# Layer 0's up projection in seven products for eight, and the w_down sums of both layers in DRAM

## The chip, the cores and the metric

The kernel runs on one core of a Trainium2 chip. The metric is the device time of one execution in microseconds (us); lower is better. The engines of the core are TensorE (PE, its weight loads PEld), VectorE (DVE), ScalarE (ACT), GpSimd (POOL) and SyncE (SP); each runs its own queue in order, and DMAs are issued from the queues of SP, ACT and POOL.

## What is computed

One inference step through two post-norm layers on 640 tokens (128 of a prompt, 512 of a sample), width 1024. Each layer modulates its input, mixes it (a state-space scan, a short convolution and an attention, which this change leaves alone), projects it with w_out, normalises, and runs an MLP of 4096 hidden columns with a squared ReLU. All data is float32.

```python
def trunk_layer(x, mod, p, lam_init, theta, prefix_k, prefix_v, s0_f, s0_b):
    sh1, sc1, g1, sh2, sc2, g2 = jnp.split(mod, 6, axis=-1)
    u = x * (1.0 + sc1) + sh1
    m, k, v, s_f, s_b = mixer(u, p, lam_init, theta, prefix_k, prefix_v, s0_f, s0_b)
    x = layer_norm(ALPHA * x + g1 * m, p['ln1_g'], p['ln1_b'])
    h = x * (1.0 + sc2) + sh2
    f = jnp.square(jax.nn.relu(h @ p['w_up'])) @ p['w_down']
    x = layer_norm(ALPHA * x + g2 * f, p['ln2_g'], p['ln2_b'])
    return x, k, v, s_f, s_b
```

The modulation vectors `mod` are a product of a conditioning vector with w_mod (1024 by 6144 per layer).

## The kernel before

Tokens stand in five tiles of 128. Every float32 product is made of three float32r products: each operand is split into a high part (ScalarE rounds it) and a low part (VectorE subtracts), and TensorE adds high x high, high x low and low x high in PSUM. `XH` and `XL` hold the two parts of the transposed activations, 8 blocks of 128 channels by 640 tokens.

Weights come from DRAM by SP into three `raw` tiles of 128 x 1024 and are split into units `hi`/`lo` (five of each in the pool `wp`), two blocks of 128 rows by 512 columns per unit.

The MLP goes through the hidden columns in groups. In layer 1 (`fast`) there are eight groups of 512; in layer 0 four groups of 1024. A group has an up projection, whose result is squared and split into `ah`/`al`, and a w_down run over five token tiles and two halves of 512 output columns.

- Layer 0: `up_block` and `ch_block`, dense, tokens in pieces of 384 and 256; the square's high part is cast on VectorE (line 1254, `V.tensor_copy`). `tok_block` runs w_down one half of columns after the other. `ev_dn` copies the first group's product into `acc[t]` in SBUF on ScalarE and adds the others on VectorE (line 1482).
- Layer 1: the first group is dense too, in two halves of 320 tokens; then `token_sums` and `token_sums_in_place` make sums and differences of the four quarters of the activations (halves of the tokens by halves of the channels), and each later group is two calls of `fast_pair`. A pair makes 256 hidden columns by seven products of 4 x 3 matmuls of 320 columns (with weight differences T1 to T4, built and split on VectorE and ScalarE) in place of eight. `dn_fast` does the w_down run: the first four items (token tile, half of columns) are half done for a start, then finished one by one; PSUM banks alternate between the pools `mm` and `tp`.

After the last group's up projection `acc` is multiplied by the gate row `grow` and added to ALPHA x `res` (two VectorE operations of 128 x 1024 per token tile); the last w_down run adds to `res` by `residual`, then comes the layer norm. The tiles `acc[0]` and `acc[1]` also hold the rows of the layer norm (`norm_rows`), the pool `gr` holds two gate rows, loaded by ScalarE's queue.

In layer 0 a generator, `mod_steps_sum`, works out the modulation of layer 1 (seven pieces of 1024 columns of w_mod) beside the MLP: SP loads 128 x 512 tiles `ws` into three buffers, VectorE multiplies and adds each into two accumulators `ma` (line 109), and per piece four matmuls `pmod`, a copy `mrow` and four transposes `pmt` end it. `spread(FU)` after each up eviction and `spread(FD)` after each w_down eviction move the generator on by that many steps; `fill_all` drains it. Its VectorE instructions carry a lower priority by LATE = 100 places.

The order on each engine's queue is fixed ahead of the run by a scheduler that goes by program order and these priorities. A tile with n buffers makes its next writer wait until the one n before has been used up.

Of the kernel before, what the change touches and what calls it, by code (L numbers as in the profile page):

```python
# [35 lines left out]
FZ, FU, FD = 2, .7, 3  # L36
# [5 lines left out]
LATE, EARLY = 100, 50  # L42
# [3 lines left out]
ORDER, N_HALF = (4, 3, 0, 1, 2), 4  # L46
# [12 lines left out]
def build(ctx: ExitStack, tc: tile.TileContext, I, O):  # L59
# [159 lines left out]
    def mod_steps_sum(pieces, pool):  # L219
# [4 lines left out]
        def small(name):  # L224
            return pool.tile([P, 4, P], F32, tag="u", name=name, bufs=3).rearrange("p a b -> p (a b)")
# [11 lines left out]
        for l, pc in pieces:  # L237
            acc = [pool.tile([P, 1024], F32, tag="xn", name=f"ma{l}_{pc}_{s}", bufs=2) for s in range(2)]
# [51 lines left out]
    def fill_all():  # L290
        while fillers:
            fill()
# [166 lines left out]
    xspill = dp.tile([TOK, D], F32, name="xspill")  # L459

# [154 lines left out]
    for l in range(DEPTH):  # L615
# [533 lines left out]

        def norm_rows(i):  # L1150
            out = []
            for j in range(2):
                r = acc[j]
# [62 lines left out]
        ubufs[0] = 5 if l + 1 == DEPTH else 3  # L1216
# [10 lines left out]
        if l + 1 < DEPTH:  # L1227
            next_end = ctx.enter_context(ExitStack())
            ep = next_end.enter_context(tc.tile_pool(name=f"kv{l + 1}", bufs=1, side=side_of(None), reuse_waits="tile"))
        op, op_end = open_pool("op")  # L1230
# [10 lines left out]
        extra = {} if fast else {"more": op, "early": EARLY}  # L1241
# [5 lines left out]
        def squared(r, hv, lv, src=None):  # L1247
# [3 lines left out]
            if fast:  # L1251
                act(hv, r)
            else:
                V.tensor_copy(hv, r)
# [5 lines left out]
        def up_block(g, b, ah, al):  # L1260
            blk = load_block(f"up{l}_{g}_{b}", w_up, 0, [(g * hg + b * 512, 512)], **extra)

            def ev_up(ct, half, ps):
                nm = f"relu{l}_{g}_{b}_{ct}_{half}"
                if fast:
                    o, m, r = half * H, H, room(nm)
                else:
                    o, m = (0, NA) if half == 0 else (NA, NB)
                    r = op.tile([P, NA], F32, tag="relu", name=nm, bufs=3)[:, :m]
# [3 lines left out]
            ch_block(f"up{l}_{g}_{b}", blk, ev_up, na=H if fast else NA)  # L1273
# [63 lines left out]
        def fast_pair(g, j, ah, al):  # L1337
# [32 lines left out]
            b = unit(1, op, 2, "c")  # L1370
# [13 lines left out]
            def out(r, ct, half, src=None):  # L1384
                o = H * half
                squared(r, ah[i + ct][:, o:o + H], al[i + ct][:, o:o + H], src)
# [25 lines left out]
        def dn_fast(g, stat, blks, evs):  # L1412

            items = [(t, c) for c in range(2) for t in ORDER]
            if g == ng - 1:
                items.sort(key=lambda x: ORDER.index(x[0]))
# [22 lines left out]

        ends = []  # L1440
        for g in range(ng):
            ah, al = a_tiles(g, hg // P)
            if fast and g:
                for j in range(2):
                    fast_pair(g, j, ah, al)
                if g == ng // 2:
                    gate_rows(1)
            else:
                for b in range(hg // 512):
                    up_block(g, b, ah, al)  # L1450
                    if g == 0 and b == 0:
                        with tc.high_priority(offset=-LATE if fast else 0):
                            for t, mv in later:
                                affine(rows, t, mv)
                        if fast:
                            with tc.high_priority(offset=-LATE):
                                token_sums()
                    if g == ng // 2 and b == 0:
                        gate_rows(1)
                if fast:  # L1460
                    token_sums_in_place()
            if g == ng - 1:
                for t in range(NT):
                    tt(acc[t], acc[t], grow[min(t, 1)], ALU.mult)
# [112 lines left out]
```

## Time and profile before

| | us |
|---|---|
| median of 3 runs | 1599.15 |
| lowest, highest run | 1598.96, 1604.01 |
| the profiled execution, its own time | 1600.18 |
| the profiled execution, its span | 1598.4 |
| TensorE busy in the span | 1558.9 |
| VectorE busy in the span | 1165.1 |
| ScalarE busy in the span | 768.6 |
| GpSimd busy in the span | 38.5 |

The profile is of one execution; the span runs from its first to its last instruction, and 1.8 us lie around it. Busy time is the time in which an engine executes an instruction. The granted clock of TensorE is full in almost all of the span. The MLP of layer 0 runs from about 392 to 841 us of the span, that of layer 1 from about 1167 us to the end.

### The profile page before, as it was taken

Reading aid. Unit: us, or ns where it says so; the run is one execution under the profiler, and the core shown is the slowest. Engines: PE = TensorE matmul, PEld = TensorE weight load, DVE = VectorE, ACT = ScalarE, POOL = GpSimd, SP = SyncE. Lnnn points to the kernel's source line nnn. Section 1 sums busy time; section 2 is a strip of 40 time slices with the busy share of each in tenths; the row PEclk is TensorE's granted clock in tenths of the full one; section 3 lists DMA queues with packets and bytes.
Section 4 is the critical chain, followed back from the end, with each engine's and each line's share of the span. In section 5 each row is a group of like instructions: output and inputs, shape, how many; then the busy total and the mean of one; then the engine's idle time right before and its main releaser. Section 6 shows DMA issues by size and latency. Waiting matters only on the chain.

```text
span 1598.4 us, 23756 instructions
## 1 busy us (share of the span) xinstructions
PE 1558.9 (98%) x9088; PEld 1373.1 (86%) x9088; DVE 1165.1 (73%) x2122; ACT 768.6 (48%) x1610; POOL 38.5 (2%) x68
## 2 busy tenths in 40 slices
PE   6999999999999999999999999999999999999997
PEld 3799957978989979979978999898798899988995
DVE  2589868778858478499376788898797566556687
ACT  3368735427422413314245587654486355434543
POOL 0000100000000000000000000000000000000001
PEclk9999999999999999999999999999999999999998
DMA  9641177342555355364226410524222233122311
GB/s 325 181 167 54 36 252 260 126 154 75 164 194 187 105 170 159 126 198 140 71 73 183 169 41 14 185 100 150 81 85 88 67 105 98 61 67 92 106 66 66
DMA packets 124833, 201.47 MB, mean 126 GB/s; under 512 B 10924, under 2 KB 57776, under 8 KB 124720
## 3 DMA queue, kind: packets, MB, share of 16 engines
q1 hardware_dynamic: 116592, 179.46, 35.0%
q10 hardware_dynamic: 8128, 20.50, 3.6%
q8 instruction: 71, 1.16, 0.3%
q14 instruction: 42, 0.34, 0.1%
HBM read 186.71 MB, written 13.22 MB: 125 GB/s over the span
## 4 chain that ended last, share of the span: by engine, by line
PE 86%; DVE 6%; DMA 3%; ACT 3%; issue 1%; POOL 1%; SPq 0%; DVEq 0%; ACTq 0%; POOLq 0%
PE dn_t L112 26%; PE up_c L112 15%; PE wo_t L112 4%; PE kv_t L112 4%; PE xb_c L112 4%; PE sa_c L112 3%; PE xa_c L112 3%; PE z_t L112 2%; PE pt L112 2%; PE px L1380 2%; PE px L1381 2%; PE px L1382 2%; PE dq_t L112 2%; PE pmod L112 2%; PE sb_c L112 2%; DVE res L109 1%
## 5 line engine op out<-in xcount | busy, mean ns | idle before, releaser
L112 PE MATMUL dn_t<-hdn,ah 128*128 128x512 f32 x640 | 251.2, 393 | 0.0
L112 PE MATMUL dn_t<-hdn,al 128*128 128x512 f32 x640 | 250.1, 391 | 0.0
L112 PE MATMUL dn_t<-ldn,ah 128*128 128x512 f32 x640 | 249.9, 390 | 0.0
L112 PE MATMUL up_c<-XH,hup 128*128 128x384 f32 (+2 forms) x576 | 178.3, 310 | 0.0
L112 PE MATMUL up_c<-XH,lup 128*128 128x384 f32 (+2 forms) x576 | 178.1, 309 | 0.1
L112 PE MATMUL up_c<-XL,hup 128*128 128x384 f32 (+2 forms) x576 | 178.1, 309 | 0.0
L109 DVE SCALAR_TENSOR_TENSOR ma<-ws,cstat,ma 128x512 f32<-128x512 f32 x196 | 138.1, 745 | 15.8 <-DMA ws<-in_w_mod_dram 15.1
L112 PEld LDWEIGHTS dn_t<-hdn,ah 128*128 128x128 f32 x640 | 120.2, 188 | 29.9 <-issue 2.5
L112 PEld LDWEIGHTS dn_t<-ldn,ah 128*128 128x128 f32 x640 | 120.2, 188 | 25.9
L112 PEld LDWEIGHTS dn_t<-hdn,al 128*128 128x128 f32 x640 | 120.2, 188 | 24.7
L112 PEld LDWEIGHTS up_c<-XH,lup 128*128 128x128 f32 x576 | 108.9, 189 | 0.8 <-DVE lup L100 0.7
L112 PEld LDWEIGHTS up_c<-XH,hup 128*128 128x128 f32 x576 | 108.1, 188 | 1.0 <-ACT relu L97 0.8
L112 PEld LDWEIGHTS up_c<-XL,hup 128*128 128x128 f32 x576 | 108.1, 188 | 0.5 <-DVE XL L100 0.2
L97 ACT ACTIVATE hdn<-rdn 128x1024 fp32r<-128x1024 f32 x64 | 66.9, 1053 | 79.7 <-PE dn_t L112 52.4
L100 DVE TENSOR_TENSOR ldn<-rdn,hdn 128x1024 fp32r<-128x1024 f32 x64 | 77.4, 1222 | 37.8 <-ACT hdn L97 37.7
L100 DVE TENSOR_TENSOR acc<-acc,dn_t 128x512 f32<-128x512 f32 x80 | 54.6, 683 | 56.5 <-PE dn_t L112 56.5
L97 ACT ACTIVATE relu<-up_c 128x384 f32<-128x384 f32 (+2 forms) x72 | 31.3, 434 | 112.1 <-PE up_c L112 105.0
L112 PE MATMUL wo_t<-hwo,XH 128*128 128x512 f32 x160 | 63.1, 394 | 1.5 <-ACT XH L97 1.5
L112 PE MATMUL wo_t<-hwo,XL 128*128 128x512 f32 x160 | 63.7, 398 | 0.0
L112 PE MATMUL wo_t<-lwo,XH 128*128 128x512 f32 x160 | 63.7, 398 | 0.0
L97 ACT ACTIVATE pe<-sc,zs 128x640 f32<-128x640 f32 (+1 forms) x80 | 56.8, 712 | 10.9 <-DVE pe L109 6.9
L844 DVE TENSOR_REDUCE zs<-sc 128x1 f32<-128x640 f32 x64 | 52.3, 820 | 12.5 <-PE sc L112 12.1
(413 smaller groups left out, 3913.2 us busy)
## 6 DMA issues: line engine op xcount, KB each, us to landing
rup<-in_w_up_dram SPq DMA_DIRECT2D x64, 512.0 KB
rdn<-in_w_down_dram SPq DMA_DIRECT2D x64, 512.0 KB
ws<-in_w_mod_dram SPq DMA_DIRECT2D x112, 256.0 KB
wm<-in_w_mod_dram SPq DMA_DIRECT2D x24, 512.0 KB
Ab<-adram SPq DMA_DIRECT2D x10, 1024.0 KB
rwo<-in_w_out_dram SPq DMA_DIRECT2D x16, 512.0 KB
wb<-in_w_mod_dram SPq DMA_DIRECT2D x12, 512.0 KB
kd<-hlks SPq DMA_DIRECT2D x40, 128.0 KB
```

The source lines that it names most:

```text
L97: S.activation(out=out, in_=in_, func=func, **kw)
L100: V.tensor_tensor(out=out, in0=a, in1=b, op=op)
L109: V.scalar_tensor_tensor(out=out, in0=a, scalar=s, in1=b, op0=op0, op1=op1, **kw)
L112: T.matmul(out, lhsT=l, rhs=r, start=start, stop=stop)
L844: V.tensor_reduce(out=nmax, in_=sv, axis=AX.XY, op=ALU.max, negate=True)
L1380: T.matmul(ps, lhsT=wh, rhs=xh, start=k == 0 and not more, stop=False, skip_group_check=more)
L1381: T.matmul(ps, lhsT=wh, rhs=xl, start=False, stop=False, skip_group_check=more)
L1382: T.matmul(ps, lhsT=wl, rhs=xh, start=False, stop=k == 3, skip_group_check=more)
```

## The change

Layer 0 goes the way of layer 1: eight groups of 512 hidden columns, the first dense in halves of 320 tokens, the other seven by `fast_pair`, w_down by one `dn_block` for both layers (the token order is 0 to 4 in layer 0 and, as before, 4, 3, 0, 1, 2 in layer 1). The square's high part is made on ScalarE in both layers.

The sums of w_down leave SBUF: in groups 0 to 6 of both layers each product of 128 x 512 is copied by ScalarE into a tile `part` (three buffers in layer 1, two in layer 0) and sent from GpSimd's queue to `accd` in DRAM, plainly in group 0 and with an accumulating DMA after that. Between the two pairs of the last group, `before_last` drains the generator, loads the second gate rows from GpSimd's queue, reads `accd` back tile by tile, folds it into `res` and loads the second norm rows.

The pool `gr` is gone: gate rows, norm rows and the sums read back share the tag `row` with two buffers; the second gate rows use the generator's tag `ma`. The generator's loads get a tag of their own, `ws`, its accumulators `ma`. The generator moves 2.1 steps per w_down eviction and none per up eviction. The weights of layer 0 no longer use a fourth unit from the pool `op`.

```diff
-FZ, FU, FD = 2, .7, 3
+FZ, FU, FD = 2, 0, 2.1
-LATE, EARLY = 100, 50
+LATE = 100
-ORDER, N_HALF = (4, 3, 0, 1, 2), 4
+ORDERS, N_HALF = ((0, 1, 2, 3, 4), (4, 3, 0, 1, 2)), 4
...
         def small(name):
-            return pool.tile([P, 4, P], F32, tag="u", name=name, bufs=3).rearrange("p a b -> p (a b)")
+            return pool.tile([P, 512], F32, tag="ws", name=name, bufs=3)
...
-            acc = [pool.tile([P, 1024], F32, tag="xn", name=f"ma{l}_{pc}_{s}", bufs=2) for s in range(2)]
+            acc = [pool.tile([P, 1024], F32, tag="ma", name=f"ma{l}_{pc}_{s}", bufs=2) for s in range(2)]
...
+    accd = dp.tile([TOK, D], F32, name="accd")
...
-        gp, gp_end = open_pool("gr", "right")
...
+        op, op_end = open_pool("op")
...
             for s in range(2):
-                r = gp.tile([P, D], F32, tag=f"grow{s}", name=f"grow{l}_{i}_{s}")
-                nc.scalar.dma_start(out=r, in_=gdram[l][i, s:s + 1, :].to_broadcast([P, D]))
+                r = op.tile([P, D], F32, tag=("row", "ma")[i], name=f"grow{l}_{i}_{s}", bufs=2)
+                (nc.scalar, G)[i].dma_start(out=r, in_=gdram[l][i, s:s + 1, :].to_broadcast([P, D]))
...
+        def row_tile(name):
+            return op.tile([P, D], F32, tag="row", name=name, bufs=2)
...
-                r = acc[j]
+                r = row_tile(f"row{l}_{i}_{j}")
...
-        acc = [op.tile([P, D], F32, name=f"acc{l}_{t}") for t in range(NT)]
         rows = norm_rows(0)
-        fast = l + 1 == DEPTH
-        ng = 8 if fast else 4
+        end = l + 1 == DEPTH
+        order = ORDERS[end]
+        ng = 8
...
             act(r, r, AF.Square)
-            if fast:
-                act(hv, r)
-            else:
-                V.tensor_copy(hv, r)
+            act(hv, r)
             tt(lv, r, f(hv), ALU.subtract)
...
+        def before_last():
+
+            nonlocal rows
+            if l + 1 < DEPTH:
+                fill_all()
+            gate_rows(1)
+            for t in order:
+                a = row_tile(f"acc{l}_{t}")
+                G.dma_start(out=a, in_=accd[t * P:(t + 1) * P, :])
+                tt(a, a, grow[min(t, 1)], ALU.mult)
+                stt(res[t], res[t], ALPHA, a, ALU.mult, ALU.add)
+            rows = norm_rows(1)
+            if l + 1 < DEPTH:
+                make_aff(l + 1, 0, vt[:, 75:83], vt[:, 83:91])
...
-            if fast and g:
+            if g:
                 for j in range(2):
                     fast_pair(g, j, ah, al)
-                if g == ng // 2:
-                    gate_rows(1)
+                    if g == ng - 1 and j == 0:
+                        before_last()
...
-                    if g == 0:
-                        act(acc[t][:, cs], ps)
-                        spread(FD)
-                    elif g < ng - 1:
-                        tt(acc[t][:, cs], acc[t][:, cs], ps, ALU.add)
+                    if g < ng - 1:
+                        part = op.tile([P, 512], F32, tag="part", name=f"part{l}_{g}_{cbi}_{t}", bufs=3 if end else 2)
+                        act(part, ps)
+                        dst = accd[t * P:(t + 1) * P, cs]
+                        if g == 0:
+                            G.dma_start(out=dst, in_=part)
+                        else:
+                            G.dma_start(out=dst, in_=part, accum_op=ALU.add)
                         spread(FD)
...
-                if fast:
-                    ends.append((blk, ev_dn))
-                else:
-                    tok_block(f"dn{l}_{g}_{cbi}", blk, a_stat, ev_dn)
-            if fast:
-                dn_fast(g, a_stat, [e[0] for e in ends], [e[1] for e in ends])
-                del ends[:]
+                ends.append((blk, ev_dn))
+            dn_block(g, a_stat, [e[0] for e in ends], [e[1] for e in ends])
+            del ends[:]
```

## Rows read from the trace of the kernel before

**Rows 1.** The page's first part: busy us (share) and instructions of each engine.
```profile
PE 1558.9 (98%) x9088; PEld 1373.1 (86%) x9088; DVE 1165.1 (73%) x2122; ACT 768.6 (48%) x1610; POOL 38.5 (2%) x68
```

**Rows 2.** Stretches: length, busy us (count) by engine, TensorE clock, DMA share, GB/s.
```profile
392.41:495.24 102.83, 102.83 (x584) 90.74 (x584) 74.34 (x123) 36.67 (x64) 0.00 (x0) 1.00 0.53 167
...
495.24:609.71 114.47, 114.47 (x650) 102.43 (x650) 80.73 (x134) 32.59 (x53) 0.00 (x0) 1.00 0.48 152
...
609.71:724.94 115.23, 114.79 (x649) 102.37 (x649) 86.16 (x137) 31.74 (x51) 0.00 (x0) 1.00 0.51 162
...
724.94:841.31 116.37, 115.28 (x662) 103.54 (x662) 78.60 (x126) 45.41 (x80) 1.62 (x3) 1.00 0.29 93
...
1274.42:1326.54 52.12, 52.12 (x291) 47.17 (x290) 31.32 (x51) 24.14 (x48) 0.00 (x0) 1.00 0.25 81
```

**Rows 3.** Chain that ended last, both MLPs: start us, us, what, count.
```profile
495.24 56.53 PE up_c L112 x384
...
1246.94 27.49 PE dn_t L112 x120
...
1299.06 27.48 PE dn_t L112 x120
```

**Rows 4.** Groups by shape (xcount | busy us, mean ns), one layer-1 group.
```profile
L100 DVE TENSOR_TENSOR lo_T<-t,hi_T 128x512 fp32r<-128x512 f32 x8 | 5.2, 686 | 2.8 <-ACT hi_T L97 2.8
...
L100 DVE TENSOR_TENSOR al<-u,ah 128x320 fp32r<-128x320 f32 x2 | 1.0, 487 | 0.1
```

**Rows 5.** Groups by shape, VectorE, layer 0's MLP (366 to 841 us).
```profile
L109 DVE SCALAR_TENSOR_TENSOR ma<-ws,cstat,ma 128x512 f32<-128x512 f32 x196 | 138.1, 745 | 15.8 <-DMA ws<-in_w_mod_dram 15.1
...
L100 DVE TENSOR_TENSOR lup<-rup,hup 128x1024 fp32r<-128x1024 f32 x30 | 36.6, 1219 | 6.1 <-ACT hup L97 6.0
...
L100 DVE TENSOR_TENSOR al<-relu,ah 128x384 fp32r<-128x384 f32 x32 | 17.6, 553 | 0.4
...
L100 DVE TENSOR_TENSOR acc<-acc,dn_t 128x512 f32<-128x512 f32 x20 | 13.6, 680 | 4.9 <-PE dn_t L112 4.9
...
L100 DVE TENSOR_TENSOR al<-relu,ah 128x256 fp32r<-128x256 f32 x32 | 13.6, 424 | 0.9
...
L1254 DVE CAST ah<-relu 128x384 fp32r<-128x384 f32 x32 | 11.3, 355 | 27.1 <-ACT relu L97 27.0
...
L1254 DVE CAST ah<-relu 128x256 fp32r<-128x256 f32 x32 | 9.3, 290 | 24.9 <-ACT relu L97 24.9
```

**Rows 6.** Groups by shape, VectorE, first group of layer 1's MLP.
```profile
L100 DVE TENSOR_TENSOR Sl<-xa,Sh 128x320 fp32r<-128x320 f32 x4 | 1.9, 484 | 0.4 <-ACT Sh L97 0.4
```

**Rows 7.** Stretches of 40 us, columns as in rows 2.
```profile
680.00:720.00 40.00, 39.98 (x181) 31.93 (x180) 37.13 (x55) 4.85 (x5) 0.00 (x0) 1.00 0.65 203
...
1160.00:1200.00 40.00, 39.00 (x247) 36.84 (x246) 37.57 (x71) 33.02 (x67) 2.59 (x2) 1.00 0.30 95
```

**Rows 8.** Timeline of a layer-1 group: start us, us, engine, line, what [idle before].
```profile
1253.85 0.69 DVE L100 TENSOR_TENSOR acc<-acc,dn_t 128x512 f32<-128x512 f32 x1 [2.13 <-PE dn_t L112]
...
1271.71 0.69 DVE L100 TENSOR_TENSOR acc<-acc,dn_t 128x512 f32<-128x512 f32 x1 [2.06 <-PE dn_t L112]
...
1272.85 1.15 ACT L97 ACTIVATE hi_b<-rup 128x512 fp32r<-128x512 f32 x2 [11.21 <-PE dn_t L112]
...
1274.26 0.31 PE L1380 MATMUL px<-XH,hi_b 128*128 128x320 f32 x1
```

**Rows 9.** DMAs: a store, a load issued and used, a full stretch.
```profile
1005.08 4.44 DMA t_new_state_ssm_bwd_dram<-sf
...
477.35 0.33 SPq L232 DMA_DIRECT2D ws<-in_w_mod_dram  x1
...
475.91 10.13 DVE L109 SCALAR_TENSOR_TENSOR ma<-ws,cstat,ma 128x512 f32<-128x512 f32 x14 [2.02 <-DMA ws<-in_w_mod_dram]
...
473.92:476.00 2.08, 2.08 (x11) 1.73 (x10) 0.09 (x1) 0.00 (x0) 0.00 (x0) 1.00 0.98 361
```

**Rows 10.** Groups by shape, ScalarE, second quarter of layer 0's MLP.
```profile
L97 ACT ACTIVATE acc<-dn_t 128x512 f32<-128x512 f32 x1 | 0.6, 576 | 0.0
```

More of the change, by code (lines that the diff above doesn't have):

```diff
@@ L1136, in build @@
         p1_end.close()
-        gp, gp_end = open_pool("gr", "right")
+        if l + 1 < DEPTH:
+            next_end = ctx.enter_context(ExitStack())
+            ep = next_end.enter_context(tc.tile_pool(name=f"kv{l + 1}", bufs=1, side=side_of(None), reuse_waits="tile"))
+        op, op_end = open_pool("op")
         grow = []
@@ L1226, in build @@
         tok_block(f"wo{l}_0", blk, x_stat, ev_o0)
[L1227 to L1230, printed above, removed]
         blk = load_block(f"wo{l}_1", w_out, 0, [(512, 512)], sc)
@@ L1260, in up_block @@
         def up_block(g, b, ah, al):
-            blk = load_block(f"up{l}_{g}_{b}", w_up, 0, [(g * hg + b * 512, 512)], **extra)
+            blk = load_block(f"up{l}_{g}_{b}", w_up, 0, [(g * hg + b * 512, 512)])
             def ev_up(ct, half, ps):
                 nm = f"relu{l}_{g}_{b}_{ct}_{half}"
-                if fast:
-                    o, m, r = half * H, H, room(nm)
-                else:
-                    o, m = (0, NA) if half == 0 else (NA, NB)
-                    r = op.tile([P, NA], F32, tag="relu", name=nm, bufs=3)[:, :m]
+                o, m, r = half * H, H, room(nm)
                 squared(r, ah[4 * b + ct][:, o:o + m], al[4 * b + ct][:, o:o + m], ps)
                 spread(FU)
-            ch_block(f"up{l}_{g}_{b}", blk, ev_up, na=H if fast else NA)
+            ch_block(f"up{l}_{g}_{b}", blk, ev_up, na=H)
         quarter = {}
@@ L1369, in fast_pair @@
                     w[n] = b[0][:, e], b[1][:, e]
-            b = unit(1, op, 2, "c")
+            b = unit(1, op, 2 if end else 1, "c")
             act(b[0][:, 0], b22)
@@ L1384, in out @@
             def out(r, ct, half, src=None):
+                spread(FU)
                 o = H * half
@@ L1410, in fast_pair, with dn_block @@
             out(room("c21" + nm), 0, 1, px)
-        def dn_fast(g, stat, blks, evs):
-            items = [(t, c) for c in range(2) for t in ORDER]
+        def dn_block(g, stat, blks, evs):
+            items = [(t, c) for c in range(2) for t in order]
             if g == ng - 1:
-                items.sort(key=lambda x: ORDER.index(x[0]))
+                items.sort(key=lambda x: order.index(x[0]))
             def part(i, ps, k0, k1):
@@ L1451, in build @@
                     if g == 0 and b == 0:
-                        with tc.high_priority(offset=-LATE if fast else 0):
+                        with tc.high_priority(offset=-LATE):
                             for t, mv in later:
                                 affine(rows, t, mv)
-                        if fast:
[L1456 to L1464, printed above, removed]
-                    stt(res[t], res[t], ALPHA, acc[t], ALU.mult, ALU.add)
-                rows = norm_rows(1)
-                if l + 1 < DEPTH:
-                    fill_all()
-                    make_aff(l + 1, 0, vt[:, 75:83], vt[:, 83:91])
+                        with tc.high_priority(offset=-LATE):
+                            token_sums()
+                token_sums_in_place()
             for cbi in range(2):
-                blk = load_block(f"dn{l}_{g}_{cbi}", w_down, g * hg, [(cbi * 512, 512)], nu=hg // 256, **extra)
+                blk = load_block(f"dn{l}_{g}_{cbi}", w_down, g * hg, [(cbi * 512, 512)], nu=hg // 256)
                 cs = slice(cbi * 512, (cbi + 1) * 512)
@@ L1498, in ev_dn @@
                             if l + 1 == DEPTH:
[L1499 to L1509 removed]
+                                final = t == order[-1]
+                                with tc.high_priority(offset=0 if final else -LATE):
+                                    finish(rows, 2 if final else 1)
+                ends.append((blk, ev_dn))
+            dn_block(g, a_stat, [e[0] for e in ends], [e[1] for e in ends])
+            del ends[:]
         if l + 1 < DEPTH:
```

12 lines of the change are left out of this document (3 added, 9 removed).

## The prediction

> **What bounds the kernel now.** I read the totals first, then the stretches of the two MLPs, then the chain that ended last in them, then the groups of VectorE. TensorE is busy 98% of the span [rows 1]. In the MLP of layer 0 it is idle for 1.5 us of 448.9 and in a group of layer 1 for nothing [rows 2], and the chain there is made of long runs of its own instructions [rows 3]. So only fewer or shorter matmuls can shorten these stretches, as long as everything that feeds TensorE keeps up. VectorE is the one to watch: the four stretches of layer 0's MLP hold 74.3 + 80.7 + 86.2 + 78.6 = 319.8 us of it, 71% of the time, where a group of layer 1 has 31.3 of 52.1 us, 60% [rows 2].
>
> **Part 1, seven products for eight in layer 0: what TensorE saves.** A dense up-projection of 1024 hidden columns is 384 matmuls in 56.53 us, so 28.27 us for 512 [rows 3]. The seven-product form is there to be read in layer 1: from one w_down run to the next is 1299.06 - 1246.94 = 52.12 us, of which the run takes 27.49, so two pairs cost 24.63 us for the same 512 columns [rows 3] (168 matmuls for 192, at the same 0.147 us each). A group saves 3.64 us; seven of the eight groups change, the first stays dense: 7 x 3.64 = 25.5 us. The first group's 320-token halves for 384 and 256 have the same columns, so nothing there. w_down keeps its matmuls. Layer 0's MLP would go from 448.9 to 423.4 us if TensorE alone counted.
>
> **What VectorE has to do for it.** Out go, in layer 0 [rows 5]: the 20 adds into acc, 13.6 us; the 64 casts of the squares (now ScalarE's), 11.3 + 9.3 = 20.6; 28 of the 32 low parts of the w_up units, 28 x 1.219 = 34.1; and 7/8 of the low parts of the squares, 7/8 x (17.6 + 13.6) = 27.3. Together 95.6 us. In come 14 pairs. Each has 11 ops 512 wide (4 differences of weights, 7 low parts) of 0.686 us and 7 ops 320 wide (3 sums of products, 4 low parts) of 0.487 us [rows 4]: 7.55 + 3.41 = 10.96 us, 153.4 for 14. The token sums are 56 ops of 0.484 us, 27.1 us [rows 6]. So 319.8 - 95.6 + 180.5 = 404.7 us of VectorE must fit into 423.4 us, 96%. The modulation work beside it (196 multiply-adds of 0.745 us, the largest item [rows 5]) stays; it is only spread over 70 evictions at 2.1 steps each, 147 for its 134 steps, in place of 30 at 3 and 64 at 0.7.
>
> Does VectorE reach 96%? The two fullest 40 us slices that I found hold 37.57 and 37.13 us, 93.4% on average, with TensorE busy 39.00 and 39.98 of 40 [rows 7]. At 93.4% the 404.7 us take 433.3 us: 9.9 us more than TensorE's 423.4. The bounds: nothing (the durations overlap a little at their ends, and VectorE could run full), and all of the 25.5 us if it only gets to 90% (404.7 / 0.90 = 449.7). I take 9.9, because the two slices are the nearest rows. The net gain is 25.5 - 9.9 = 15.6 us. ScalarE takes over the casts and 60 of the evictions, about 0.58 us each [rows 10]; at 48% of the span [rows 1] it has room, unless it is made to wait.
>
> **Part 2, the sums in DRAM.** Per layer 70 evictions become a ScalarE copy into a "part" tile and a 256 KB DMA from POOL's queue, 60 of them accumulating; five 512 KB loads bring the sums back. In layer 1 this takes 60 adds of about 0.69 us from VectorE [rows 8], but TensorE is busy through those groups [rows 2], so layer 1 gains nothing. The cost is a new wait: a copy needs a free part tile (2 in layer 0, 3 in layer 1), which is free once its DMA has landed. Behind a waiting copy on ScalarE's queue stands the next pair's hi_b, on which TensorE waits.
>
> The limit can be worked out from a group of layer 1. Its w_down run starts at 1246.94 [rows 3]; the first eviction starts 6.9 us later, the ninth is due at 1271.71, hi_b is computed at 1272.85 when the last unit of weights comes free, and its matmul starts at 1274.26 [rows 8]. As hi_b takes 0.58 us for its first half, there are 0.83 us of room, so the ninth copy must end by 26.7 us after the start. With two tiles the ninth waits for the seventh, fifth, third and first: it ends at 6.9 + 4 x (0.58 + L) + 0.58 at the earliest, where L is the DMA from issue to landing. That is in time up to L = 4.2 us; above it every us of L costs 4 us a group, 28 us over seven groups. With three tiles (third eviction near 9.7, as the first four tiles end six matmuls of 0.229 us apart) the same sum gives 9.7 + 2 x (0.58 + L) + 0.58, in time up to 7.6 us.
>
> No accumulating DMA and none issued from POOL is in this trace. From below: a 256 KB load with the same 2 KB rows, issued at 477.35 into the third tile behind, was used without a wait by the fourth pair of multiply-adds of a row of 14 in 10.13 us, at 475.91 + 3 x 1.447 = 480.25, so it took at most 2.9 us [rows 9]. From above: that load and a 256 KB store of 4.44 us [rows 9] one after the other, 7.3 us. I take 3.6: the load's shape is nearest, and the second read of 256 KB adds 0.73 us at the 361 GB/s that the engines moved when 98% busy [rows 9]. That is under both limits, so it costs nothing here; the upper end would cost layer 0 3.1 x 28 = 87 us.
> The Trainium skill, "Collectives: The Full Stack", section "The bandwidth ceiling: the fold count and why AG ≠ RS ≠ AR", says that an add inside a DMA is slow not for the add but because it needs two source reads, which halves the rate. No run here shows it. Taken for the bytes alone it is the 0.73 us just added; taken for the whole 2.9 us of the load, L would be 5.8 us and the result 1583.6 + 1.6 x 28 = 1628 us by that page, inside rival 2 below.
>
> **Part 3, the rest.** The gate rows and norm rows share two "row" tiles with the five sums read back, and the second gate rows go to POOL's queue into the two "ma" tiles. So on POOL: the loads wait behind the gate rows, and those wait until the modulation has given up its "ma" tiles; the layer norm's powers stand behind all of them. On ScalarE, the two norm-row DMAs wait until the last sums have been folded into res. The sums are folded 12 us before w_down of the last group starts; the first residual follows 6.9 us into that run, some 19 us in all. The loads need three rounds of two; with about 4 us for 512 KB (estimate, the load above and 0.73 us more) and 2.4 us of VectorE as before, 19 us. It fits with nothing to spare, and the fifth is due later. I take 0, with 0 to 5 us per layer as bounds. The new order of the last run by token tile, as layer 1 has it, I cost at nothing, within 2 us either way. The earlier opening of pools: nothing.
>
> **Sum.** The profiled execution took 1600.2 us with a span of 1598.4; the median of the runs is 1599.15, 1.0 lower. 1600.2 - 25.5 + 9.9 = 1584.6, and 1.0 less for the median: 1583.6 us.
>
> **Rivals.** (1) VectorE becomes the bound altogether. For it: 96% needed, in-order queues, the modulation's matmuls standing in TensorE's queue, and group 0, where 27 us of token sums [rows 6] and a seventh of the modulation, some 21 us [rows 5], come on top of its own splits in about 56 us. Against: the modulation may slip by 100 places. At 90% the gain is gone: 1599; at 91 to 88%, 1594 to 1609. (2) The other side: the two part tiles are too few. Place: ScalarE's copy ahead of hi_b in layer 0's groups 1 to 7; price 28 us per us of L over 4.2; it decides from L = 4.2 + 15.6 / 28 = 4.76 us. For it: the store of 4.44 us, and DMA engines half busy in layer 0 already [rows 2]. Against: that store had shorter rows, and if the schedule puts hi_b ahead of the copy the limit is about 1 us higher. At L = 5 it gives 1606, at 6 1634, at 7.3 1671. (3) The change gives more than TensorE's share less the loss, because VectorE runs full: 1574 to 1576.
>
> **How the numbers follow.** Forecast (VectorE at 92 to 95%, L under 4.5): 1576 to 1594, chance 0.58, and full gain (3) 0.05. Rival 1: 0.17, most of it from 1594 to 1604. Rival 2: 0.20, from 1604 up, a fifth of it under 1606. The range 1573 to 1606 leaves out most of rival 2 and the tail of rival 1, together 0.2. A measurement of this kernel can tell about 0.3%, 4.8 us, from no change. Faster than 1594.4: 0.58 + 0.05 = 0.63. Within: 0.11 of rival 1. Slower than 1603.9: 0.06 of rival 1 and 0.20 of rival 2, 0.26.
>
> **What would show it.** Right: layer 0's groups with a period of 52 to 54 us, px in place of up_c, VectorE at 92% or more there, layer 1's period still 52.1, and no idle TensorE ahead of px. Wrong by rival 1: idle TensorE released by lo_T, lo_b or p, with VectorE busy all the time. Wrong by rival 2: ScalarE idle, released by the DMA that writes accd, and TensorE idle ahead of px by several us in each group of layer 0. Wrong in part 3: TensorE idle in the last group of a layer, ahead of the first residuals.

## The result: 3.5% slower, and the profile after

The median of the changed kernel is 1657.43 us (1649.41 to 1661.19), that of the kernel before, on the same chip, 1599.56 us: a ratio of 1.0349, 95% interval 1.0303 to 1.0395. 1583.6 us was forecast, at most 1606. The runs of the changed kernel lie up to 12 us apart; its profiled execution took 1649.41 us, with a span of 1647.5, so it is 49 us longer than the one of before. Where a few us decide, I read them from the traces.

Lines of the page after: busy time by engine [rows 1], and three groups of instructions (busy us, mean ns | idle time before them, what ended it).

```profile
PE 1555.3 (94%) x8920; PEld 1361.5 (83%) x8920; DVE 1190.0 (72%) x2202; ACT 900.7 (55%) x1922; POOL 162.8 (10%) x222
...
L97 ACT ACTIVATE part<-dn_t 128x512 f32<-128x512 f32 x140 | 82.2, 595 | 202.9 <-DMA accd<-part 114.4
L1484 POOL DMA_DIRECT2D accd<-part x120 | 103.6, 898 | 564.8 <-ACT part L97 544.2
L109 DVE SCALAR_TENSOR_TENSOR ma<-ws,cstat,ma 128x512 f32<-128x512 f32 x196 | 138.4, 744 | 26.9 <-DMA ws<-in_w_mod_dram 26.7
```

TensorE has 168 matmuls less and is busy for 3.6 us less only, and ScalarE's copies stand 114.4 us behind accumulating DMAs. Four of six periods of layer 0's MLP (from one w_down run to the next; the sum is over all six) and one of layer 1, columns as in [rows 2]:

```profile
472.53:532.06 59.53, 54.93 (x303) 47.63 (x301) 47.28 (x79) 30.10 (x61) 8.62 (x10) 1.00 0.75 195
...
652.45:719.05 66.60, 58.08 (x302) 51.18 (x301) 47.25 (x79) 29.94 (x61) 8.60 (x10) 0.92 0.70 178
719.05:781.63 62.58, 55.99 (x303) 49.11 (x302) 45.38 (x78) 28.52 (x59) 8.59 (x10) 0.97 0.68 163
781.63:847.26 65.63, 57.70 (x292) 49.95 (x290) 34.94 (x50) 30.22 (x61) 12.53 (x17) 0.90 0.67 162
sum 374.73, PE 336.35 PEld 292.96 DVE 268.08 ACT 177.01 POOL 55.52; mean PE 56.06 PEld 48.83 DVE 44.68 ACT 29.50 POOL 9.25
...
1288.28:1340.40 52.12, 52.12 (x290) 47.17 (x289) 25.57 (x42) 29.67 (x59) 8.69 (x10) 1.00 0.62 131
```

Layer 1's period is unchanged at 52.12 us, as in [rows 2]. In layer 0 TensorE is idle for 374.73 - 336.35 = 38.4 us of these six periods, and its clock falls to 0.90 to 0.97 in the last three. VectorE is busy for 47 of 60 and of 67 us: it is not full. The landing times say why (GpSimd's issues that write accd, duration in ns; then the time from issue to landing), for plain and accumulating DMAs of layer 0, then of layer 1:

```profile
L1482 POOL DMA_DIRECT2D accd<-part x10: 539/539/742, 423.7 to 445.1; - x10
DMA to landing us min/median/max: 2.3/2.7/6.0
...
L1484 POOL DMA_DIRECT2D accd<-part x60: 838/857/961, 480.6 to 820.6; - x60
DMA to landing us min/median/max: 3.6/5.1/8.7
...
L1482 POOL DMA_DIRECT2D accd<-part x9: 539/542/594, 1246.9 to 1265.2; - x9
DMA to landing us min/median/max: 2.3/2.3/4.8
...
L1484 POOL DMA_DIRECT2D accd<-part x60: 847/860/1476, 1298.4 to 1580.7; - x60
DMA to landing us min/median/max: 3.5/4.6/6.5
```

An accumulating DMA lands after 5.1 us in layer 0. The limit worked out for two part tiles was 4.2. The waits of the layer 0 MLP (414 to 850 us; us in total, times, longest) show two followers:

```profile
ACT part L97 <- DMA accd<-part: 101.8, 41, 6.7
...
DVE ma L109 <- DMA ws<-in_w_mod_dram: 26.7, 24, 2.9
```

The first follower is the one of rival 2, ScalarE's copies. The second was not in the prediction: VectorE stands on late loads of w_mod, and what is queued behind the standing multiply-add, the differences of weights t of the next pair, is late too. This is one such place, from the timeline of VectorE, ScalarE and TensorE:

```profile
688.62 1.41 DVE L109 SCALAR_TENSOR_TENSOR ma<-ws,cstat,ma 128x512 f32<-128x512 f32 x2 [0.93 <-DMA ws<-in_w_mod_dram]
692.05 0.75 DVE L109 SCALAR_TENSOR_TENSOR ma<-ws,cstat,ma 128x512 f32<-128x512 f32 x1 [2.01 <-DMA ws<-in_w_mod_dram]
692.71 1.29 DVE L100 TENSOR_TENSOR lo_b<-rup,hi_b 128x512 fp32r<-128x512 f32 x2
693.92 3.40 DVE L109 SCALAR_TENSOR_TENSOR ma<-ws,cstat,ma 128x512 f32<-128x512 f32 x5
697.23 0.68 DVE L100 TENSOR_TENSOR t<-rup 128x512 f32<-128x512 f32 x1
...
688.79 0.60 ACT L97 ACTIVATE part<-dn_t 128x512 f32<-128x512 f32 x1 [2.44 <-DMA accd<-part]
...
697.95 0.63 ACT L97 ACTIVATE hi_T<-t 128x512 fp32r<-128x512 f32 x1 [7.21 <-DVE t L100]
698.49 0.42 ACT L97 ACTIVATE u<-px 128x320 f32<-128x320 f32 x1
...
698.96 0.64 PE L1375 MATMUL px<-XH,hi_T 128*128 128x320 f32 x1 [5.18 <-ACT u L97]
```

VectorE is held twice by loads, then works off five multiply-adds whose data has come, and only then forms t. ScalarE stands 7.21 us on it with the copy u queued behind hi_T, and px waits 5.18 us on u.

In layer 1 most of the time goes into the last group: its pairs take 31.6 us in place of 24.63 (29.71 for 156 of their 168 matmuls and 1.86 for the other 12, behind three of w_down), and TensorE is idle for 5.27 of them. GpSimd's queue holds the first load of the sums back behind DMAs not yet landed, VectorE stands on that load, and t is late again:

```profile
1572.08 0.56 POOL L1444 DMA_DIRECT2D acc<-accd  x1 [4.60 <-DMA accd<-part]
...
1576.39 1.23 DVE L100 TENSOR_TENSOR acc<-acc,grow 128x1024 f32<-128x1024 f32 x1 [10.38 <-DMA acc<-accd]
...
1587.84 0.63 ACT L97 ACTIVATE hi_T<-t 128x512 fp32r<-128x512 f32 x1 [7.31 <-DVE t L100]
```

So of the 49 us: layer 0's MLP starts 5.5 us late (383.58 for 378.07 us), it loses 33 us where 25.5 were to be won, and layer 1 loses the rest, about 11 us: some 7 in its last group and 3 in the up projection of its first (34.4 us for 31.4 before).

### The profile page after: what moved, and what is told of

It reads as the page before. It is cut to its first block, busy times and chain, and to the rows that moved or that the text cites. A ratio compares the mean times of both kernels' runs of the same rounds, so it can differ in the third digit from the quotient of the medians.

```text
span 1647.5 us, 24250 instructions
## 1 busy us (share of the span) xinstructions
PE 1555.3 (94%) x8920; PEld 1361.5 (83%) x8920; DVE 1190.0 (72%) x2202; ACT 900.7 (55%) x1922; POOL 162.8 (10%) x222
## 4 chain that ended last, share of the span: by engine, by line
PE 38%; issue 38%; DVE 7%; POOL 7%; DMA 6%; ACT 2%; SPq 1%; POOLq 0%; DVEq 0%; ACTq 0%
POOL accd L1484 6%; PE sa_c L112 4%; PE xb_c L112 3%; PE dn_t L112 3%; PE kv_t L112 3%; PE wo_t L112 3%; PE xa_c L112 2%; PE up_c L112 2%; PE pt L112 2%; PE z_t L112 2%; PE dq_t L112 2%; PE sb_c L112 1%; PE sc L112 1%; PE pmod L112 1%; PE pt L859 1%
## 5 line engine op out<-in xcount | busy, mean ns | idle before, releaser
L97 ACT ACTIVATE part<-dn_t 128x512 f32<-128x512 f32 x140 | 82.2, 595 | 202.9 <-DMA accd<-part 114.4
L1484 POOL DMA_DIRECT2D accd<-part x120 | 103.6, 898 | 564.8 <-ACT part L97 544.2
L109 DVE SCALAR_TENSOR_TENSOR ma<-ws,cstat,ma 128x512 f32<-128x512 f32 x196 | 138.4, 744 | 26.9 <-DMA ws<-in_w_mod_dram 26.7
L100 DVE TENSOR_TENSOR lo_T<-t,hi_T 128x512 fp32r<-128x512 f32 x112 | 74.0, 686 | 84.2 <-ACT hi_T L97 76.5
L1375 PE MATMUL px<-XH,hi_T 128*128 128x320 f32 x224 | 73.2, 327 | 21.6 <-ACT u L97 20.3
L97 ACT ACTIVATE hi_T<-t 128x512 fp32r<-128x512 f32 x112 | 67.1, 626 | 48.0 <-DVE t L100 45.6
L1376 PE MATMUL px<-XL,hi_T 128*128 128x320 f32 x224 | 71.5, 319 | 0.0
L1377 PE MATMUL px<-XH,lo_T 128*128 128x320 f32 x224 | 71.5, 319 | 0.0
L100 DVE TENSOR_TENSOR lo_b<-rup,hi_b 128x512 fp32r<-128x512 f32 x56 | 37.0, 685 | 46.4 <-ACT hi_b L97 46.3
L1375 PEld LDWEIGHTS px<-XH,hi_T 128*128 128x128 f32 x224 | 44.1, 197 | 24.8 <-ACT u L97 21.8
```

The lines of the kernel that those rows point to most:

```text
L97: S.activation(out=out, in_=in_, func=func, **kw)
L100: V.tensor_tensor(out=out, in0=a, in1=b, op=op)
L109: V.scalar_tensor_tensor(out=out, in0=a, scalar=s, in1=b, op0=op0, op1=op1, **kw)
L1375: T.matmul(ps, lhsT=wh, rhs=xh, start=k == 0 and not more, stop=False, skip_group_check=more)
L1376: T.matmul(ps, lhsT=wh, rhs=xl, start=False, stop=False, skip_group_check=more)
L1377: T.matmul(ps, lhsT=wl, rhs=xh, start=False, stop=k == 3, skip_group_check=more)
```

## The experiments

My theory from this trace: the landing time of the accumulating DMAs makes the loss, through the wait for part tiles (rival 2). The rivals to it: VectorE is the bound (rival 1); or the DMAs delay other transfers. Medians in us; the kernel before, run beside them, had 1598.5 to 1600.2. e2, e3 and e5 leave work out, as the table says, so their results are not the reference's: they measure and are no alternatives.

| run | what differs from the changed kernel | median |
|---|---|---|
| e1_four_parts | layer 0: four part buffers | 1638.8 |
| e2_plain_dma | plain DMAs for accumulating: sums left out | 1614.3 |
| e3_copy_only | no DMA in groups 1 to 6: sums left out | 1601.6 |
| e4_layer1_sbuf | layer 1's sums in SBUF | 1640.0 |
| e5_four_no_ws | e1, loads of w_mod left out but for two | 1596.3 |
| e6_two_parts_l1 | layer 1: two part tiles | 1661.9 |
| e7_two_in_sbuf | e4, two of five sums of layer 0 in SBUF | 1608.2 |
| e8_two_in_sbuf_spread | e7, modulation spread over the pairs | 1610.7 |
| e12_two_parts_ws_five | e4, five ws buffers | 1625.2 |
| e9_ws_five | e12, four part buffers | 1600.9 |
| e9h_ws_five_held | e9, first loads held back | 1617.0 |
| e10_two_in_sbuf_held | e7, first loads held back | 1623.0 |
| e13_ws_five_late | e9, multiply-adds 300 places back | 1603.5 |
| e14_ws_five_spread | e9, modulation spread over the pairs | 1598.5 |
| e16_t_on_pool | e14, t on GpSimd | 1632.5 |
| e17_first_on_act | e14, first products on ScalarE | 1606.2 |

**The part tiles alone.**

```diff
+                        if not end and g and (5 * cbi + t) % 2:
+                            part = row_tile(f"part{l}_{g}_{cbi}_{t}")[:, :512]
+                        else:
                             part = op.tile([P, 512], F32, tag="part", ...)
```

> In layer 0, groups 1 to 6, every second eviction copies into one of the two row tiles (idle there), so four buffers serve where two did; nothing else differs from the changed kernel (1657 us). Theory W (the copies on ScalarE wait for part tiles whose accumulating DMA, 5.1 us in the median, has not landed): with four buffers the ninth copy waits only above some 10 us, so layer 0's periods fall from 58 to 66 us to 53 to 55 us and the whole to 1595 to 1612 (layer 1's extra 8 to 15 us stay). Theory V (VectorE cannot do the work of seven products and modulation together): still 1635 or more.

Measured: 1638.8 us, 19 less than the changed kernel. The waits of layer 0's MLP:

```profile
DVE ma L109 <- DMA ws<-in_w_mod_dram: 39.0, 19, 4.7
ACT part L97 <- DMA accd<-part: 19.9, 14, 2.8
```

ScalarE's wait went from 101.8 to 19.9 us, and the w_down runs are back at 29 to 31 us. VectorE's wait for ws went from 26.7 to 39.0, and the pairs of groups 1 to 6, counted from 0, take 184 us in place of the 6 x 24.63 = 148 that TensorE needs (the expectation of e5 counts these groups from 1). In the timeline of one of them hi_b is long done, but lo_b and t stand behind multiply-adds:

```profile
616.92 1.15 ACT L97 ACTIVATE hi_b<-rup 128x512 fp32r<-128x512 f32 x2 [0.53 <-PE dn_t L112]
...
624.20 1.41 DVE L109 SCALAR_TENSOR_TENSOR ma<-ws,cstat,ma 128x512 f32<-128x512 f32 x2 [3.68 <-DMA ws<-in_w_mod_dram]
625.53 1.28 DVE L100 TENSOR_TENSOR lo_b<-rup,hi_b 128x512 fp32r<-128x512 f32 x2
...
631.77 0.64 PE L1375 MATMUL px<-XH,hi_T 128*128 128x320 f32 x1 [6.27 <-ACT u L97]
```

The theory holds for the first follower and is not the whole: the wait moved to VectorE's queue. By its time alone the run falls where theory V was expected, 1635 or more; e5 below decides between VectorE's work and its waits.

**The DMAs themselves.** e2 drops `accum_op`, e3 the DMAs of groups 1 to 6.

```diff
-                            G.dma_start(out=dst, in_=part, accum_op=ALU.add)
+                            G.dma_start(out=dst, in_=part)
```

> All 120 accumulating DMAs become plain ones of the same size to the same place (the sums over groups are left out). Theory W: the plain DMAs of group 0 landed in 2.7 us in the median, under the limit of 4.2, so the waits go: 1585 to 1605. Theory V: no effect on VectorE, 1635 or more. A third reading, that any DMA from POOL's queue costs as much by itself: 1635 or more with ScalarE still waiting.

> In groups 1 to 6 of both layers the product is copied into the part tile and goes nowhere (these sums are left out); group 0's store and the reading back stay. No copy ever waits. Theory W: the forecast's own case, 1576 to 1594. Theory V: VectorE's work is all there, so 1635 or more. What is left above 1574 is VectorE's share and the ends of the layers.

Measured: 1614.3 and 1601.6, both above what was expected of theory W. The add inside the DMA is worth 43 us of the changed kernel's time, the remaining transfers 13; the plain DMAs still hold ScalarE's copies for 47.8 us in layer 0's MLP. GpSimd's issues and landing in e2, layer 0 and then layer 1:

```profile
L1484 POOL DMA_DIRECT2D accd<-part x56: 539/539/756, 478.3 to 776.9; - x56
DMA to landing us min/median/max: 2.3/3.6/6.6
...
L1484 POOL DMA_DIRECT2D accd<-part x50: 539/539/556, 1315.0 to 1542.9; - x50
DMA to landing us min/median/max: 2.3/2.3/5.7
```

3.6 us is what I had taken for L; it is the time of the plain DMA beside this traffic. e3 alone left it open why no gain remained without any of these DMAs. In its trace layer 0's MLP starts at 383.05 us, 5 late, some 8 us go by the first of its fast groups, and 8 in the first pairs of layer 1's MLP (32.24 us, 24.64 in e5 and e9); that last item is e3's own, and I did not follow it up.

**Layer 1's sums.** The adds of the kernel before, in layer 1 alone.

```diff
+                    if g < ng - 1 and end:
+                        if g == 0:
+                            act(acc[t][:, cs], ps)
+                        else:
+                            tt(acc[t][:, cs], acc[t][:, cs], ps, ALU.add)
...
```

> Layer 1 keeps its sums in SBUF with adds on VectorE, as in the kernel before; layer 0 is that of the changed kernel. The trace of the changed kernel has layer 1 slower by 5 us in its last group (sums read back late) and 2.6 us at its end. Theory that these come from the sums in DRAM: 1642 to 1652. Theory that they only follow from layer 0's lateness or other placement: no change, 1649 to 1661.

Measured: 1640.0; 17 us by the medians, 9 by the profiled executions; from the start of its MLP to the end of the span layer 1 takes 436.1 us for 445.7. The last pairs take 24.76 us again. Sums in DRAM cost layer 1 time and give nothing.

**VectorE's work, or its waits?** e5 leaves the loads out and keeps every multiply-add.

```diff
-            if loads:
+            if len(fixed) == 2 and loads:
+                at = loads.pop(0)
+                got[at] = fixed[at[3]]
+            elif loads:
...
```

> The four part buffers of e1, and the 128x512 loads of w_mod left out: the modulation's multiply-adds all run, but read two tiles that were loaded once (so the modulation of layer 1 is not the reference's). VectorE has as many instructions as in e1; its waits for loads are gone, and the DMA engines carry less. e1 took 1638.8 us. Theory A (the stalls of the pairs come from VectorE standing in order on loads that the accumulating DMAs hold up): the pairs of layer 0's groups 2 to 7 go from 184 us in all to about 152, as in e3, and the time to 1605 to 1615. Theory B (the work of VectorE itself, in its order, is what makes the pairs late): the pairs stay over 175 us and the time over 1630.

Measured: 1596.3, a ratio of 0.9987 (0.9971 to 1.0004) to before, and 42 us under e1: theory A, with more than it had promised. One period and five in a row of layer 0, columns as above:

```profile
465.18:518.76 53.58, 53.58 (x302) 47.61 (x301) 46.96 (x79) 29.94 (x60) 8.67 (x10) 1.00 0.61 128
...
465.18:733.63 268.45, 268.32 (x1504) 238.08 (x1502) 230.96 (x391) 148.93 (x295) 43.04 (x50) 1.00 0.61 128
```

With VectorE busy for 230.96 of 268.45 us, 86%, TensorE is never idle. The work of VectorE fits; that kills rival 1 for these groups. The period of 53.6 us is the one that step 1 of the sum wants, and layer 1's MLP begins 16.4 us earlier than before (1146.84 for 1163.23). The start of layer 0's MLP is back as well, 378.52 us, with the multiply-adds beside w_out still there: it was the loads issued there (16 from 320 to 371 us in the changed kernel, two in e5), not VectorE's work.

The whole is only 4 us below the kernel before because e5 keeps layer 1's sums in DRAM: from the start of layer 1's MLP to the end of the span it takes 445.5 us, for 435.2 before, and TensorE stands in the last group as in the changed kernel:

```profile
1533.40 0.64 PE L1381 MATMUL px<-XH,hi_T 128*128 128x320 f32 x1 [6.38 <-ACT u L97]
```

Layer 0's last group is not free of waits either: TensorE stands 2.49 us for VectorE's p there, and the chain that ends last goes through two loads of the sums. Without layer 1's 10 us e5 would come near the forecast; that sum was not run.

**The rule for two part tiles, in a place without modulation.**

```diff
-                        part = op.tile(..., bufs=3 if end else 2)
+                        part = op.tile(..., bufs=2)
```

> Layer 1 with two part tiles instead of three, nothing else changed; layer 1 has no modulation beside its MLP, so this is the prediction's rule alone. The rule (ninth copy ends 6.9 + 4 (0.58 + L) + 0.58 us after the start of w_down, in time up to L = 4.2 us) with the measured median of L = 4.6 us: 1.6 us a group, period 52.1 to 53.7 us, 11 us in all over the 1657 (1649 at the lowest) of the changed kernel. If the rule is right but single DMAs of 5 to 6.5 us count: 3 to 5 us a group, 20 to 35 us. Rival (hi_b stands ahead of the last copies, or copies are not what TensorE waits for): period 52.1 as with three, no change.

Measured: 1661.9; the profiled execution is 4.2 us longer than that of the changed kernel, although its layer 1 starts w_down 4.5 us earlier: from the first w_down run of layer 1 to the end of the last it takes 408.4 us for 399.7, 8.7 more. The pairs of groups 1 to 6 take 26.14, 26.68, 24.96, 24.64, 24.95 and 26.13 us for 24.63, so 0 to 2 us a group, 0.95 on average, and those of the last group 34.8 us for 31.6. The median landing is 4.2 us (3.5 to 7.1); the rule gives 0 at 4.2 and 1.6 at 4.6 us, so single late DMAs count, not the median alone. A place where it bites:

```profile
1312.41 0.60 ACT L97 ACTIVATE part<-dn_t 128x512 f32<-128x512 f32 x1 [2.77 <-DMA accd<-part]
1314.52 0.60 ACT L97 ACTIVATE part<-dn_t 128x512 f32<-128x512 f32 x1 [1.52 <-DMA accd<-part]
...
1317.28 0.60 ACT L97 ACTIVATE part<-dn_t 128x512 f32<-128x512 f32 x1 [1.12 <-DMA accd<-part]
1317.77 0.43 ACT L97 ACTIVATE s<-px 128x320 f32<-128x320 f32 x1
...
1318.26 0.41 PE L1375 MATMUL px<-Sh,hi_T 128*128 128x320 f32 x1 [1.79 <-ACT s L97]
```

The mechanism stands, and its price is of the right size. What waits is not px's start on hi_b, as I had it, but its second use on the copy s.

**Fewer DMAs in layer 0.** Two of five sums in the row tiles, on top of e4; e8 spreads the modulation as well.

```diff
+                    acc += [row_tile(f"accs{l}_{t}") for t in range(2)]
...
+                    if g < ng - 1 and (end or t < 2):
...
```

> As e4 (layer 1's sums in SBUF), and in layer 0 the sums of token tiles 0 and 1 stay in SBUF too, in the two row tiles, with VectorE's adds (28 of about 0.69 us, 19 us more for VectorE); six products of ten in a group go to DRAM, two part tiles. e4 took 1640 us. Theory A (what costs is the DMAs, by the waits of ScalarE for part tiles and of VectorE for loads): both fall by half or more, w_down runs of layer 0 at 29 to 31 us, time 1605 to 1618. Theory B (VectorE's own work, in its order): the 19 us more of it make the pairs later, time 1625 to 1645.

> As e7, with the modulation's steps spread over the pairs too: 0.9 a product of the pairs and 1.3 an eviction of w_down, in place of 0 and 2.1. If the steps packed into the w_down runs keep VectorE from the next pair's differences of weights: 5 to 12 us less than e7. If steps between the products of a pair only delay lo and p there: the same as e7 within 4 us, or up to 10 us more.

Measured: 1608.2 and 1610.7. Four DMAs of ten less and 19 us more for VectorE make the kernel 32 us faster than e4: the DMAs are what costs. Where the steps are put makes no difference.

**Time for the loads to land.** e12 and e9, both with layer 1 as in e4. The products go into the row tiles, and the freed 4 KB are two more ws buffers.

```diff
-            return pool.tile([P, 512], F32, tag="ws", name=name, bufs=3)
+            return pool.tile([P, 512], F32, tag="ws", name=name, bufs=5)
...
```

> As e9_ws_five (five buffers for the loads of w_mod, layer 1's sums in SBUF), but two part buffers in layer 0 instead of four. The prediction's rule with a landing of 4.6 to 5.1 us: 4 (L - 4.2) = 1.6 to 3.6 us a group, six accumulating groups, 10 to 22 us: 1611 to 1623 us against e9's 1601. If the copies' waits are the cause of everything and the late loads only their follower: 1630 or more. If they cost nothing once the loads are early: 1598 to 1604.

> Layer 1's sums in SBUF as in e4; in layer 0 the evicted products go into the halves of the two row tiles (room for four), the tag part is gone there, and its 4 KB make the buffers of w_mod's loads five instead of three. All ten products of a group go to DRAM. e1 (four parts) and e4 together, if their gains of 18.7 and 17.4 us add, would be 1621 us. Theory A (VectorE's order is broken by loads of w_mod that land late: with two more buffers a load has two more steps, about 3 us, to land): waits of VectorE for ws fall from e1's 39 us in layer 0's MLP to under 10, pairs under 27 us on average, time 1592 to 1608. Rival (the loads are short of bandwidth, not of time: more buffers only shift the wait): ws waits over 25 us, time 1615 to 1625.

Measured: 1625.2 with two part buffers, 1600.9 with four. The same two waits as above, e12:

```profile
ACT part L97 <- DMA accd<-part: 84.5, 38, 6.9
...
DVE ma L109 <- DMA ws<-in_w_mod_dram: 4.2, 6, 1.2
```

and e9:

```profile
ACT part L97 <- DMA accd<-part: 11.1, 3, 4.4
...
DVE ma L109 <- DMA ws<-in_w_mod_dram: 8.0, 7, 1.9
```

This separates the three causes, one edit at a time: 1657.4 (the changed kernel), 1640.0 (layer 1's sums in SBUF, 17.4), 1625.2 (loads in time, 14.8), 1600.9 (four part tiles, 24.3). The sizes hang on the order: four part tiles alone gave 19 us (e1), and layer 1's step is 9 by the profiled executions. The part tiles alone cost 4 us a group, and e12's w_down runs show it: 34.9, 35.0, 34.0, 34.7, 30.5 and 33.4 us for 29.0. The rule gives 4 x (5.1 - 4.2) = 3.6 us for the changed kernel's landing of 5.1, and 2.8 for the 4.9 that is the median in e12 (3.6 to 8.5).

**What is left.** e9 is level with the kernel before (1.0014, 0.9999 to 1.0028), not 25 us faster. Its layer 1 MLP begins at 1159.91 us, 3.3 earlier; 3.8 us are lost at the start of layer 0's MLP, 11.5 in its groups 1 to 6 (467.46 to 775.87 us holds six runs of 28.97 and five times two pairs of 24.62, 296.9 of 308.4 us), the rest in its first and last groups. e9h and e10 hold the loads beside w_out back.

```diff
+        for i in range(5):
+            V.tensor_copy(small(f"hold{i}")[:, 0:1], gate[0])
...
```

> As e9_ws_five, and the generator's first loads are held back until the first group's up projection has written its first square (one column is copied from it into each ws buffer first). In the changed kernel 15 loads of w_mod and 27 multiply-adds run beside w_out, and the MLP of layer 0 starts 5.5 us later than before. If these loads are the cause: its start is back at 378 to 379 us of the span and the time 4 to 6 us under e9, less what the 27 multiply-adds (18 us of VectorE) cost later. Rival (the start is late for the order of the row tiles): start stays at 383 to 385, no gain.

> As e7 (layer 1 and two of five sums of layer 0 in SBUF), with the same hold on the generator's first loads. e7 took 1608.2 us, its MLP of layer 0 started at 385.0 us of the span. If the loads beside w_out are the cause of the late start: 378 to 379 us, and the time 1601 to 1606, since the 27 multiply-adds that ran early there now have to run in the MLP. Rival: start 383 to 385 and 1608 or more.

Measured: 1617.0 and 1623.0, 16 and 15 us more than e9 and e7. The start is back at 379.32 and 377.16 us, as the theory had it, but the price was missed: the 27 multiply-adds that had run beside w_out come into groups 0 and 1, where there is no room, and the modulation's own matmuls stand in TensorE's queue for them (TensorE's timeline in e9h):

```profile
456.49 3.90 PE L112 MATMUL pmod<-ma,one 128*32 128x512 f32 x8 [4.61 <-DVE ma L109]
```

In that form rival 1 is alive: VectorE's work of the first two groups does not fit. Three more edits to VectorE's order or load followed.

> As e9_ws_five, with the modulation's multiply-adds 300 places back instead of 100 in the order that the scheduler makes. If what is left in e9's pairs (11 us over seven groups, TensorE waiting on u and p) is multiply-adds ahead of the differences of weights on VectorE's queue: 3 to 8 us less, 1593 to 1598. Rival (they have to be done anyway, and later they collide with the modulation's own matmuls): the same within 3 us, or up to 10 us more.

> As e9_ws_five, with the modulation's steps spread over the pairs as well (0.9 a product, 1.3 an eviction of w_down, in place of 0 and 2.1). If clumps of loads and multiply-adds in the w_down runs are what is left: 3 to 8 us less than e9's 1600.9. If the order that the scheduler makes evens them out already, as e7 and e8 suggest: the same within 4 us.

> As e14 (1598.5 us), with layer 0's differences of weights t worked out by GpSimd instead of VectorE: 56 operations, 38 us less for VectorE, and t no longer queued behind multiply-adds that wait for loads. If VectorE's order is what is left: 4 to 10 us less, 1588 to 1595. Rival: GpSimd's subtraction is slower than VectorE's 0.686 us (not shown so far) and stands behind its own accumulating DMAs, which wait for ScalarE's copies, so t comes later: 1605 or more.

> As e14 (1598.5 us), with the first product of each modulation piece (one of eight multiply-adds) on ScalarE instead of VectorE: 28 operations of 0.48 us, 13 us less for VectorE over layer 0. If VectorE's work is what is left, about a third of it comes back as time: 3 to 5 us less. Rival: ScalarE then waits for loads and for the modulation's matmuls in its own order: the same or up to 6 us more.

Measured: 1603.5, 1598.5 (1.0004, 0.9987 to 1.002), 1632.5 and 1606.2. None gains beyond the spread of the runs. GpSimd takes 1.63 to 1.85 us for a difference that VectorE forms in 0.69, so the differences come late in e16 and TensorE waits 28 us for p. GpSimd's groups there:

```profile
L1361 POOL TENSOR_TENSOR t<-rup,t 128x512 f32<-128x512 f32 x28 | 45.5, 1625 | 16.0 <-DMA rup<-in_w_up_dram 15.3
L1361 POOL TENSOR_TENSOR t<-rup 128x512 f32<-128x512 f32 x14 | 25.9, 1851 | 104.2 <-DMA rup<-in_w_up_dram 102.8 <-DVE xe L100 1.4
```

e17 takes 13 us from VectorE and is slower than e14 all the same. What makes the last 11 us in e9's groups is therefore not settled. e5 shows that they go when the loads go; with five buffers VectorE waits only 8 us for them, and SyncE's queue, which carries these loads and the weights, was not tried in another arrangement. No version that computes the whole result beat the kernel before.

## Why the prediction was wrong

**Part 1, TensorE's saving: right.** 25.5 us were forecast, 3.64 a group. Where nothing waits (e5) the period is 53.6 us, for 57.2 before by the same rows (28.27 and 28.97).

**Part 1, VectorE: the size was off, to the safe side.** 404.7 us in 423.4 was 96%. e5's five periods have 86%, and TensorE was full beside it. Two reasons: the sum added durations, and successive operations overlap (five multiply-adds in 3.40 us, 0.68 each for 0.745); and with tags of their own the modulation's tiles let 27 multiply-adds start beside w_out. The second I should have read from the diff: the old tags `u` and `xn` were what kept them back. It has a price that I had costed at nothing, 5.5 us at the start of the MLP, by the loads there.

**Part 2: the step that failed.** L was taken as 3.6 us and is 5.1 in layer 0 and 4.6 in layer 1. It lay within the bounds of 2.9 to 7.3, but I took the end of a load that had no add, and put the add at the bytes' share of full bandwidth, 0.73 us. The rows now show the pair: 2.3 us plain and 4.6 accumulating in layer 1, twice as long; 3.6 (e2) and 5.1 in layer 0.
The Trainium skill, "Collectives: The Full Stack", section "The bandwidth ceiling: the fold count and why AG ≠ RS ≠ AR", says of the reduce step of a collective that its add needs two source reads, so that it runs at half the rate of a copy. Layer 1's 2.3 and 4.6 us agree with that taken for the whole time of the DMA, layer 0's factor of 1.4 with less. I had it in the text, with 1628 us as its result, and gave it a chance of 0.20 with the rest of rival 2; the trace of before held nothing against it.

**Rival 2: right in place, near in price, short in reach.** It decides from 4.76 us and gives 1606 at 5. Its 28 us per us of L count seven groups, but group 0's DMAs are plain: six, 24 us, would have been right. The part tiles cost 24 us (e12 to e9), 4 a group, where the rule gives 2.8 to 3.6. Of the 74 us between the forecast and the result these are a third. 17 more are what e9 still stands above the forecast, in part open; the others were not in rival 2:

- The loads of w_mod land late when the DMA engines carry the sums (their share is 0.75 in the first period above, 0.48 to 0.53 in three of four stretches before [rows 2]; VectorE's wait for them is 26.7 us here, 11.0 in e3 without those DMAs); three buffers gave them too little time. 15 us (e4 to e12). VectorE was asked about as a quantity of work, not as a queue in which a late load holds everything behind it.
- Layer 1's last group, 5 us of idle TensorE, and 9 to 17 us for its sums in DRAM in all (e4). Part 3 had 0, with 5 as its bound, and "the fifth is due later"; it is the first load that is late, held by DMAs that had not landed.
- The clock, below.

**"What would show it".** ScalarE released by the DMA on accd came as written for rival 2. TensorE's idle time came ahead of px's later products, on s and u, and ahead of the modulation's matmuls, not only ahead of its start.

## What to carry to other kernels

When sums move into accumulating DMAs, ask for the landing time of that very kind of DMA before counting buffers; with only a plain one to go by, take twice its time (the factors here were 2.0 and 1.4). Then list every other stream that needs the DMA engines in the same stretch and the engine that waits for it in order: buffers for that stream (here two of 256 KB, 15 us) are part of the price. A tile that gets a tag of its own also loses a wait that kept its work in place, so look where that work goes.

## What the runs showed of the hardware

- An accumulating DMA of 256 KB from GpSimd's queue holds that queue for 0.86 us, a plain one for 0.54.
- Behind some waits TensorE's granted clock falls to 0.50, the lower of its two levels (1.2 GHz). Two stretches of the changed kernel right after a wait, of 5.18 and 4.92 us, and what followed the first:

```profile
698.96:704.00 5.04, 5.04 (x19) 5.04 (x20) 5.04 (x10) 4.30 (x9) 0.00 (x0) 0.50 0.37 137
704.00:719.05 15.05, 15.05 (x103) 15.05 (x102) 12.68 (x21) 10.14 (x21) 0.00 (x0) 0.99 0.62 208
...
829.15:834.00 4.85, 4.84 (x18) 4.85 (x19) 4.84 (x9) 3.01 (x6) 0.55 (x1) 0.50 0.37 115
```

19 matmuls in 5 us, where the next 15 us hold 103: such a stall costs half as much again. The length of the wait alone does not settle it: right behind waits of 2.87 and 3.98 us the clock is 0.56 and 0.54 (670.11 to 674.00 and 762.25 to 766.00 us), behind one of 3.23 us 1.00 (555.56 to 560.00 us), behind layer 1's 5.27 us 0.72 (1588.85 to 1594.00 us). In the last three of the six periods TensorE is busy for 58.08, 55.99 and 57.70 us, 11.0 us more in all than 3 x 53.59, beside the 38.4 us of idle time in the six. In the first three, at a clock of 1.00, it is 3.8 us more, which no run explains.
